# Hybrid decoder layer: the first up-projection weights are cast behind the last tiles of h, and two output-weight tiles change places

## The chip, the cores and the metric

The kernel runs on one core of one Trainium2 chip. The metric is the device time of one execution in microseconds (us); less is better. The engines are named as in the profile: PE is TensorE (matmuls; PEld its weight loads), DVE VectorE, ACT ScalarE, POOL GpSimd, SP SyncE, which here issues DMAs.

## The reference, cut to what matters

One decoder layer on S = 1024 tokens of width D = 1024, in float32:

```python
xn = rmsnorm(x, attn_norm_g)
proj = xn @ w_in                      # queries, keys, values of two head groups, forget logits
out_a = sliding-window attention with sinks (8 heads)
out_b = forgetting attention (8 heads)
x = x + concat(out_a, out_b) @ w_out  # this sum is h
hn = rmsnorm(x, mlp_norm_g)
x = x + square(relu(hn @ w_up)) @ w_down   # w_up: 1024 x 4096
```

## The kernel before

Everything is kept transposed: a tile of h is 128 of the 1024 features (tile number dt = 0 to 7) by 1024 tokens. The stages are the input projection with both attentions, the output projection, the up projection and the down projection. The scheduler of the framework orders each engine's instructions by a simulated timeline; `tc.issue_after(x)` is a constraint on that order only (what stands under it is put behind x), and each engine then runs its queue in order.

**Split into high and low.** Each float32 factor of a matmul is used as a high part rounded to fp32r and a low part. `split` (line 77) lets ScalarE cast the high part, and line 80 lets VectorE or POOL subtract it from the source. A product of 128 rows of the contraction is then three matmuls: high by high, high by low, low by high (line 73). In the profile `bh` and `bl` are the high and low part of h, `wos` a tile of output weights, `wu` one of up weights.

**Output projection.** `out_first` adds the products of the first four tiles of the attention's output (`mix`) to x for each dt and stores the sum in `part_d`, while the last attention units still run. The second half, over mix 4 to 7, starts with tiles 0 and 4 beside the last attention units and goes on with tiles 1, 5, 2, 6, 3, 7 (the six tiles) when the attention is done. `out_weights` loads a weight tile (`wor`), splits it with ScalarE and POOL, and puts it into one of the places w0 to w6 of the memory, by the counter `i`: tiles 0 and 4 are i = 9 and 10, then tiles 1, 5, 2, 6, 3, 7. A place can be written again when the last reader of what it held is done. `out_finish` (line 982) loads the stored part, adds the product to it (line 988: this is h), stores h to `h_d` (line 989), and splits it. h of tiles 0 to 3 lies in w2, of tiles 4 to 6 in w3, of tile 7 in `rr`. The up projection uses a Strassen-like scheme with seven products n over half-size blocks; their right-hand sides are the halves of h themselves (n = 1, 2, 3: line 977 on ScalarE, 978 on VectorE) and sums `ts` of them (n = 4 to 7: lines 995 and 1007 on VectorE, then `split`). `b12` (line 994) is a scaled copy that those sums use.

**Up projection.** For 16 column blocks j the seven products are made in the order UP = 1, 2, 3, 6, 7, 5, 4, 12 matmuls each, over four contraction tiles k. `up_weights` (line 1048) takes the next place by `w_slot` and splits; the low part is VectorE's for n = 2, 6, 5 and POOL's for n = 1, 3, 7, 4. The weights n = 1 of j = 0 and j = 1 (the first pair) are made ahead of the loop, and their products run first. `up_sum` makes the sums of raw weights (`wus`, lines 1027 and 1030), the loop's end adds the products (`u`, `hb`).

**Attention's last units.** VectorE masks the scores (line 699) with masks `cm` that POOL makes (line 694), ScalarE takes the exponential (line 704), VectorE or POOL divides (lines 713, 715), TensorE transposes the probabilities (`tpb`, line 740), and ScalarE and VectorE split them (`pth`, `ptl`).

Of the kernel before, what the change touches and what calls it, by code (L numbers as in the profile page):

```python
# [9 lines left out]
F32R = mybir.dt.float32r  # L10
BF16 = mybir.dt.bfloat16
AF = mybir.ActivationFunctionType
# [4 lines left out]
P = 128  # L17
# [12 lines left out]
NW = 7  # L30
# [25 lines left out]
def hybrid_layer(  # L56
# [13 lines left out]
    nc = tc.nc  # L70
# [4 lines left out]
    def split(hi, lo, src, hi_eng, lo_eng):  # L75
        if hi_eng is nc.scalar:
            hi_eng.copy(hi, src)  # L77
        else:
            hi_eng.tensor_copy(hi, src)
        return lo_eng.tensor_tensor(out=lo, in0=src, in1=hi.bitcast(F32), op=ALU.subtract)  # L80
# [63 lines left out]
    def slot(tag, name, shape, dt=F32, pool=None):  # L144
        pool = o[pool or ("zx" if tag == "w6" else "zw" if tag[0] == "w" else "zl")]
        return pool.tile([P] + shape, dt, tag=tag, name=name, bufs=1)
# [7 lines left out]
    def x_part(j, k, rows):  # L154

        c, r0 = divmod(rows.start, 512)
        return X[c][k // 2][:, j, k % 2, r0 : r0 + rows.stop - rows.start]
# [27 lines left out]
    for k in range(KT):  # L185
# [18 lines left out]
        for cs in pieces:  # L204
            hi, lo = (x_part(j, k, cs) for j in range(2))
# [657 lines left out]
        mix_tiles(e)  # L863
        return nc.sync.dma_start(mixt[e].bitcast(F32), mixs_d[e].rearrange("c p s -> p c s"))

    WOS = ("w5", "w6", "w0", "w1", "w5", "w6")
    nout = [0]

    def out_weights(dt, e0):
        i = nout[0] = nout[0] + 1  # L870
        wr = o["zw"].tile([P, 4, P], F32, tag="wor", name="wor", bufs=2)
        nc.sync.dma_start(wr, w_o[dt][:, e0 : e0 + 4, :])
        w = slot(WOS[i - 11] if i > 10 else f"w{i % 2}", "wos", [2, 4, P], F32R)
        split(w[:, 0], w[:, 1], wr, nc.scalar, nc.gpsimd)
        return w[:, 0], w[:, 1]

# [11 lines left out]
    def out_products(ps, w, es):  # L888
        wh, wl = w
        for e in es:  # L890
            j = e % 4
            for c in range(2):
                cs = slice(c * 512, (c + 1) * 512)
                mm(ps[c], wh[:, j, :], mh[e][:, cs], j == 0, False)
                mm(ps[c], wh[:, j, :], ml[e][:, cs], False, False)
            for c in range(2):
                cs = slice(c * 512, (c + 1) * 512)
                mm(ps[c], wl[:, j, :], mh[e][:, cs], False, j == 3)
# [73 lines left out]
    left, right = slice(0, 512), slice(512, 1024)  # L972
    part = {}

    def h_split(n, t, src, gain):
        hi, lo = bh[n][:, t, :], bl[n][:, t, :]
        nc.scalar.activation(hi, src, AF.Copy, scale=gain)  # L977
        nc.vector.scalar_tensor_tensor(  # L978
            out=lo, in0=src, scalar=gain, in1=hi.bitcast(F32), op0=ALU.mult, op1=ALU.subtract
        )  # L980

    def out_finish(dt, ps):
        t, gain = dt % 4, gm[:, dt : dt + 1]
        h = slot(f"w{2 + dt // 4}", "h", [S]) if dt < 7 else rr
        with tc.issue_after(part["load"].ins) if dt == 7 else nullcontext():
            part["load"] = nc.sync.dma_start(h, part_d[dt])
        for c, cs in enumerate((left, right)):
            nc.vector.tensor_tensor(out=h[:, cs], in0=ps[c], in1=h[:, cs], op=ALU.add)  # L988
        nc.sync.dma_start(h_d[dt], h)
        if dt < 4:  # L990
            h_split(1, t, h[:, left], gain)
            ts = part["t"] = slot("r1", "ts", [4, 512])
            b12 = part["b12"] = slot("w4", "b12", [512])
            nc.scalar.activation(b12, h[:, right], AF.Copy, scale=gain)
            nc.vector.scalar_tensor_tensor(
                out=ts[:, 0], in0=h[:, left], scalar=gain, in1=b12, op0=ALU.mult, op1=ALU.subtract
            )
            return
        ts, b12 = part["t"], part["b12"]
        h_split(2, t, h[:, left], gain)  # L1000
        h_split(3, t, h[:, right], gain)
        for i, q, other, op in (
            (1, right, ts[:, 0], ALU.add),
            (2, right, b12, ALU.subtract),
            (3, left, ts[:, 1], ALU.subtract),
        ):
            nc.vector.scalar_tensor_tensor(  # L1007
                out=ts[:, i], in0=h[:, q], scalar=gain, in1=other, op0=ALU.mult, op1=op
            )
        part["rest"] = lambda: sum_splits(ts, t, ((0, 5), (3, 4)))  # L1010
        sum_splits(ts, t, ((1, 6), (2, 7)))
        if t < 3:
            part.pop("rest")()

    def sum_splits(ts, t, which):
        for i, n in which:
            split(bh[n][:, t], bl[n][:, t], ts[:, i], nc.scalar, nc.vector)
# [3 lines left out]
    def up_load(j):  # L1021
        raws[j] = slot({0: "m3", 1: "m2"}.get(j, f"r{j % 2}"), "wur", [2, KT, P])
        for i in range(2):
            up_loads[j] = nc.sync.dma_start(raws[j][:, i], w_u[j + i * NJ])

    def minus(out, a, b, eng=nc.vector):
        eng.tensor_tensor(out=out, in0=a, in1=b, op=ALU.subtract)  # L1027

    def plus(out, a, b, eng=nc.vector):
        eng.tensor_tensor(out=out, in0=a, in1=b, op=ALU.add)  # L1030

    def up_sum(j):
        raw = raws.pop(j)
        s = slot("m5" if j % 2 == 0 else "m4" if j > 1 else "r1", "wus", [4, 4, P])
        a11, a12, a21, a22 = raw[:, 0, :4], raw[:, 0, 4:], raw[:, 1, :4], raw[:, 1, 4:]
        plus(s[:, 0], a21, a22)
        minus(s[:, 1], s[:, 0], a11)
        minus(s[:, 2], a11, a21)
        minus(s[:, 3], a12, s[:, 1])
        return {1: a11, 2: a12, 3: s[:, 3], 4: a22, 5: s[:, 0], 6: s[:, 1], 7: s[:, 2]}  # L1040

    nw = [0]

    def w_slot(name, shape, dt=F32):
        nw[0] += 1
        return slot(f"w{(0, 1, 5, 6, 2, 3, 4)[(nw[0] - 1) % NW]}", name, shape, dt)

    def up_weights(n, src):
        w = w_slot("wu", [2, 4, P], F32R)
        split(w[:, 0], w[:, 1], src, nc.scalar, nc.vector if n in (2, 6, 5) else nc.gpsimd)  # L1050
        return w
# [3 lines left out]
    for dt, ps, w in ahead_of:  # L1055
        out_finish(dt, ps)
# [7 lines left out]
    def bank(name):  # L1064
        nbank[0] += 1
        return pm.tile([P, 512], F32, tag=f"m{nbank[0] % 8}", name=name, bufs=1)

    for dt in (1, 5, 2, 6, 3, 7):
        w = out_weights(dt, 4)
        ps = [bank(f"po{c}") for c in range(2)]  # L1070
        out_products(ps, w, range(4, 8))
        out_finish(dt, ps)
        if dt == 5:
            with tc.issue_after(part["load"].ins):
                up_load(1)
        if dt == 3:
            up_ahead = [up_weights(1, up_sums[0][1]), up_weights(1, raws[1][:, 0, :4])]

# [5 lines left out]
    def up_products(n, w, ps):  # L1084
        for k in range(4):
            mm(ps, w[:, 0, k], bh[n][:, k], k == 0, False)
            mm(ps, w[:, 0, k], bl[n][:, k], False, False)
            mm(ps, w[:, 1, k], bh[n][:, k], False, k == 3)
# [3 lines left out]
    def up(j):  # L1092
        if 0 < j < NJ - 1:
            up_load(j + 1)
        src = up_sums.pop(0) if j == 0 else up_sum(j)
        m = {}
        for n in UP:
            if n == 1 and j == 1:
                m[n] = second.pop()
            else:  # L1100
                w = up_ahead.pop(0) if n == 1 and j == 0 else up_weights(n, src[n])
                m[n] = bank(f"pu{n}")
                up_products(n, w, m[n])
            if n == 1 and j == 0:
                second.append(bank("pu1"))
                up_products(1, up_ahead.pop(), second[0])
            if n == 2 and j == 0:
                part.pop("rest")()
            if n == 2 and j == 1:
                nbank[0] += 1  # L1110
            if n == 1:
                u = slot("m1", "u", [4, 512])
                b = slot("m2" if j else "m0", "hb", [4, 512])
                nc.scalar.copy(u[:, 0], m[1])
            if n == 2:
                plus(b[:, 0], m[2], u[:, 0])
            if n == 6:
                plus(u[:, 1], m[6], u[:, 0])
            if n == 7:
                plus(u[:, 2], m[7], u[:, 1])  # L1120
            if n == 5:
                minus(u[:, 3], u[:, 1], m[5])
                minus(b[:, 2], u[:, 2], m[5])
                plus(b[:, 3], m[3], u[:, 3])
            if n == 4:
                plus(b[:, 1], m[4], u[:, 2])
        return lambda: up_end(j, b)
# [207 lines left out]
    for i in range(len(STEPS)):  # L1335
        down(i)
        if STEPS[i][0] == len(PHASES) - 1 and late:
            name, dt, cs = late.pop(0)
# [65 lines left out]
```

## Time and profile before

| | |
|---|---|
| median of 3 runs | 1088.91 us (1088.80 to 1089.02) |
| the profiled execution | 1092.64 us, its span 1090.9 us |
| mean granted TensorE clock | 0.997 |
| PE, PEld busy | 99%, 86% of the span |
| DVE, ACT, POOL busy | 71%, 53%, 36% |
| place A: last attention units | about 397 to 431 us |
| place B: from the output to the up projection | about 460 to 495 us |

In the rows of the trace the first number is the start in us from the span's start, the second the duration in us, then engine, line, operation, output<-inputs, shape and a count (x2: two such in a row in one entry). What stands in brackets is the idle time of the engine just before, and what ended it. A matmul of 128x512 takes 0.39 us from start to end, but the next one starts before it has ended. Rows of the waits give the total in us, how often, and the longest. Names of buffers are cut at their numbers.

### The profile page before, as it was taken

The numbers are of one execution on the slowest core, as the hardware profiler recorded it, in microseconds if no ns is written. First come the engines' busy times: TensorE is split into PE (matmuls) and PEld (weight loads), VectorE is DVE, ScalarE is ACT, GpSimd is POOL, SyncE is SP. The second block draws the span as 40 slices with busy tenths as digits, with TensorE's granted clock in tenths as the row PEclk, the third lists the DMA queues.
The fourth block names the chain that finished last, engine by engine and source line by source line (L and its number), as shares of the span: only waits on it lengthen the run. The fifth ranks groups of instructions, "written<-read, shape, count | busy, mean of one in ns | idle before, by whom it ended". The sixth has DMA issues, their size and how long they took to land.

```text
span 1090.9 us, 15569 instructions
## 1 busy us (share of the span) xinstructions
PE 1074.9 (99%) x5492; PEld 933.1 (86%) x5492; DVE 773.2 (71%) x1319; ACT 577.0 (53%) x1022; POOL 388.8 (36%) x350
## 2 busy tenths in 40 slices
PE   9999999999999999989999999999999999999998
PEld 8999999999998887868888888888888888888886
DVE  7377787877866787887776759665675876664395
ACT  5558587776867765545545453443533433333331
POOL 4572433547456653233332232332222232131100
PEclk9999999999999999999999999999999999999999
DMA  8401112334747664643545443443998895665523
GB/s 281 168 19 57 62 46 62 116 99 128 253 155 248 230 196 169 220 172 142 193 167 202 174 164 117 147 172 145 331 390 311 308 327 190 218 234 185 176 88 115
DMA packets 96222, 195.67 MB, mean 179 GB/s; under 512 B 7392, under 2 KB 19856, under 8 KB 96144
## 3 DMA queue, kind: packets, MB, share of 16 engines
q1 hardware_dynamic: 95856, 194.54, 51.6%
q8 instruction: 43, 0.70, 0.3%
q14 instruction: 35, 0.29, 0.1%
q10 hardware_dynamic: 288, 0.15, 0.0%
HBM read 141.61 MB, written 53.04 MB: 178 GB/s over the span
## 4 chain that ended last, share of the span: by engine, by line
PE 67%; DVE 4%; DMA 3%; issue 1%; ACT 1%; SPq 0%; DVEq 0%; ACTq 0%
PE pu L73 28%; PE pd L73 28%; PE po L73 4%; PE pvb L73 2%; PE tpb L740 2%; PE spb L73 1%; DMA mix_d<-mtb 1%; PE ps L73 1%; DMA h<-part_d 1%; DMA h_d<-h 1%; DVE h L988 1%; DVE bl L978 0%; DVE ptl L403 0%; DVE ts L1007 0%; DMA mixn<-rd_d 0%
## 5 line engine op out<-in xcount | busy, mean ns | idle before, releaser
L73 PE MATMUL pd<-hx,wx 128*128 128x512 f32 (+1 forms) x1350 | 304.9, 388 | 0.0
L73 PEld LDWEIGHTS pd<-hx,wx 128*128 128x128 f32 x1350 | 252.7, 188 | 52.2
L73 PE MATMUL pu<-bh,wu 128*128 128x512 f32 x896 | 277.9, 391 | 3.6 <-ACT bh L977 3.6
L73 PEld LDWEIGHTS pu<-bh,wu 128*128 128x128 f32 x896 | 169.0, 189 | 39.4 <-ACT bh L977 4.0
L73 PE MATMUL ps<-w,x 128*128 128x384 f32 (+1 forms) x960 | 196.5, 342 | 1.1 <-POOL w L80 0.8
L73 PE MATMUL pu<-bl,wu 128*128 128x512 f32 x448 | 175.2, 391 | 0.2 <-DVE bl L978 0.2
L73 PEld LDWEIGHTS ps<-w,x 128*128 128x128 f32 x960 | 165.1, 188 | 5.3 <-POOL w L80 1.5
L77 ACT CAST hx<-hr 128x1024 fp32r<-128x1024 f32 x56 | 59.0, 1054 | 174.9 <-PE pd L73 170.6
L80 POOL TENSOR_TENSOR wx<-wda,wx 128x1024 fp32r<-128x1024 f32 x24 | 66.1, 2755 | 194.8 <-ACT wx L77 172.4
L80 DVE TENSOR_TENSOR hx<-hr,hx 128x1024 fp32r<-128x1024 f32 x56 | 77.4, 1387 | 75.7 <-ACT hx L77 75.7
L73 PEld LDWEIGHTS pu<-bl,wu 128*128 128x128 f32 x448 | 84.5, 189 | 18.3 <-DVE bl L978 0.7
L80 POOL TENSOR_TENSOR wu<-wus,wu 128x512 fp32r<-128x512 f32 x32 | 48.0, 1502 | 130.5 <-ACT wu L77 130.5
L73 PE MATMUL po<-mix,wos 128*128 128x512 f32 x384 | 93.4, 393 | 0.0
L73 PEld LDWEIGHTS po<-mix,wos 128*128 128x128 f32 x384 | 70.7, 188 | 14.0 <-ACT pc L916 0.2
L77 ACT CAST wu<-wus 128x512 fp32r<-128x512 f32 x64 | 39.3, 620 | 80.7 <-PE pu L73 73.2
L80 POOL TENSOR_TENSOR wu<-wur,wu 128x512 fp32r<-128x512 f32 x32 | 47.0, 1469 | 86.5 <-ACT wu L77 86.5
L1027 DVE TENSOR_TENSOR ht<-hb 128x512 f32<-128x512 f32 x32 | 22.9, 757 | 64.1 <-ACT hb L1131 64.1
L704 ACT ACTIVATE sb<-sb,nmb 128x128 f32<-128x128 f32 (+3 forms) x64 | 49.8, 779 | 26.8 <-DVE nmb L699 26.1
L403 DVE TENSOR_TENSOR ptl<-tpb,pth 128x512 fp32r<-128x512 f32 (+1 forms) x80 | 50.1, 631 | 18.3 <-ACT pth L402 17.9
L77 ACT CAST wx<-wda 128x1024 fp32r<-128x1024 f32 x56 | 58.5, 1049 | 8.1 <-DMA wda<-in_w_d_dram 8.1
L80 POOL TENSOR_TENSOR w<-wr,w 128x384 fp32r<-128x384 f32 (+1 forms) x47 | 49.9, 1069 | 29.6 <-ACT w L77 15.8
L694 POOL TENSOR_SCALAR_AFFINE_SELECT cm<-cb 128x128 f32<-128x128 f32 (+1 forms) x64 | 30.8, 482 | 60.2 <-DVE nmb L699 59.6
(205 smaller groups left out, 1829.9 us busy)
## 6 DMA issues: line engine op xcount, KB each, us to landing
wda<-in_w_d_dram SPq DMA_DIRECT2D x34, 1024.0 KB, 9.2
hr<-hid_d SPq DMA_DIRECT2D x56, 512.0 KB, 5.8
wur<-in_w_u_dram SPq DMA_DIRECT2D x32, 512.0 KB, 4.4
hid_d<-ht SPq DMA_DIRECT2D x16, 1024.0 KB, 4.4
hid_d<-hb SPq DMA_DIRECT2D x16, 768.0 KB, 3.9
mix<-mixs_d SPq DMA_DIRECT2D x7, 1024.0 KB, 5.7
wr<-in_w_b_dram SPq DMA_DIRECT2D x32, 192.0 KB, 2.5
xq<-in_x_dram SPq DMA_DIRECT2D x8, 512.0 KB, 5.8
```

The source lines that it names most:

```text
L73: return nc.tensor.matmul(out, lhsT, rhs, start=start, stop=stop)
L77: hi_eng.copy(hi, src)
L80: return lo_eng.tensor_tensor(out=lo, in0=src, in1=hi.bitcast(F32), op=ALU.subtract)
L403: nc.vector.tensor_tensor(out=lo[:, cols], in0=pt[:, cols], in1=hi[:, cols].bitcast(F32), op=ALU.subtract)
L694: nc.gpsimd.affine_select(out=cm, in_=bias, pattern=[[-1, n]], compare_op=ALU.is_ge, fill=BIG, base=n - P, channel_multiplier=1,)
L704: nc.scalar.activation(pr[:, :nk], pr[:, :nk], AF.Exp, scale=-1.0, bias=nm[:, c : c + 1], accum_out=dn_b[p % 2][:, h, i : i + 1] if p < 3 ...
L740: nc.tensor.transpose(tp[:, c0 : c0 + P], probs[qi][:, kb * P : (kb + 1) * P], ident)
L988: nc.vector.tensor_tensor(out=h[:, cs], in0=ps[c], in1=h[:, cs], op=ALU.add)
L1027: eng.tensor_tensor(out=out, in0=a, in1=b, op=ALU.subtract)
```

## The change

There are three edits.

1. The table WOS gets another entry in front and is read from i = 10 on. Tile 4's weights (i = 10) go to w5, which is free, where they went to w0, which tile 7's first-half weights hold; tile 1's go to w0 instead of w5; tile 5's stay in w6, tile 2's in w0 go to w1, tile 6's to w5, tile 3's to w0, tile 7's stay in w6.
2. `out_finish` keeps its last cast on ScalarE of lines 977 and 994, one for each of the six tiles in a list `casts`. In the loop's first block (j = 0) the weights of n = 2 are put behind tile 3's copy b12, and all the others behind tile 7's cast of the right half (n = 3).
3. The order of places in `w_slot` changes: the first pair uses w1 and w5, n = 2 w0, n = 3 w6, n = 6 w3 (was w2), n = 7 w4 (was w3), n = 5 w2 (was w4), n = 4 w1 (the cycle then repeats).

```diff
@@ -863,14 +863,14 @@
         mix_tiles(e)
         return nc.sync.dma_start(mixt[e].bitcast(F32), mixs_d[e].rearrange("c p s -> p c s"))
 
-    WOS = ("w5", "w6", "w0", "w1", "w5", "w6")
+    WOS = ("w5", "w0", "w6", "w1", "w5", "w0", "w6")
     nout = [0]
 
     def out_weights(dt, e0):
         i = nout[0] = nout[0] + 1
         wr = o["zw"].tile([P, 4, P], F32, tag="wor", name="wor", bufs=2)
         nc.sync.dma_start(wr, w_o[dt][:, e0 : e0 + 4, :])
-        w = slot(WOS[i - 11] if i > 10 else f"w{i % 2}", "wos", [2, 4, P], F32R)
+        w = slot(WOS[i - 10] if i > 9 else f"w{i % 2}", "wos", [2, 4, P], F32R)
         split(w[:, 0], w[:, 1], wr, nc.scalar, nc.gpsimd)
         return w[:, 0], w[:, 1]
 
@@ -974,7 +974,7 @@
 
     def h_split(n, t, src, gain):
         hi, lo = bh[n][:, t, :], bl[n][:, t, :]
-        nc.scalar.activation(hi, src, AF.Copy, scale=gain)
+        part["cast"] = nc.scalar.activation(hi, src, AF.Copy, scale=gain)
         nc.vector.scalar_tensor_tensor(
             out=lo, in0=src, scalar=gain, in1=hi.bitcast(F32), op0=ALU.mult, op1=ALU.subtract
         )
@@ -991,7 +991,7 @@
             h_split(1, t, h[:, left], gain)
             ts = part["t"] = slot("r1", "ts", [4, 512])
             b12 = part["b12"] = slot("w4", "b12", [512])
-            nc.scalar.activation(b12, h[:, right], AF.Copy, scale=gain)
+            part["cast"] = nc.scalar.activation(b12, h[:, right], AF.Copy, scale=gain)
             nc.vector.scalar_tensor_tensor(
                 out=ts[:, 0], in0=h[:, left], scalar=gain, in1=b12, op0=ALU.mult, op1=ALU.subtract
             )
@@ -1043,7 +1043,7 @@
 
     def w_slot(name, shape, dt=F32):
         nw[0] += 1
-        return slot(f"w{(0, 1, 5, 6, 2, 3, 4)[(nw[0] - 1) % NW]}", name, shape, dt)
+        return slot(f"w{(1, 5, 0, 6, 3, 4, 2)[(nw[0] - 1) % NW]}", name, shape, dt)
 
     def up_weights(n, src):
         w = w_slot("wu", [2, 4, P], F32R)
@@ -1065,6 +1065,7 @@
         nbank[0] += 1
         return pm.tile([P, 512], F32, tag=f"m{nbank[0] % 8}", name=name, bufs=1)
 
+    casts = []
     for dt in (1, 5, 2, 6, 3, 7):
         w = out_weights(dt, 4)
         ps = [bank(f"po{c}") for c in range(2)]
@@ -1073,6 +1074,7 @@
         if dt == 5:
             with tc.issue_after(part["load"].ins):
                 up_load(1)
+        casts.append(part["cast"].ins)
         if dt == 3:
             up_ahead = [up_weights(1, up_sums[0][1]), up_weights(1, raws[1][:, 0, :4])]
 
@@ -1098,7 +1100,8 @@
             if n == 1 and j == 1:
                 m[n] = second.pop()
             else:
-                w = up_ahead.pop(0) if n == 1 and j == 0 else up_weights(n, src[n])
+                with tc.issue_after(casts[-2 if n == 2 else -1]) if j == 0 else nullcontext():
+                    w = up_ahead.pop(0) if n == 1 and j == 0 else up_weights(n, src[n])
                 m[n] = bank(f"pu{n}")
                 up_products(n, w, m[n])
             if n == 1 and j == 0:
```

What this makes of the queues is shown at three places. In the names of the queues wos_5732 is tile 4's weights, wos_5913 tile 1's; wu_6142 and wu_6145 are the first pair, wu_6223 is n = 2 of j = 0, wu_6244 n = 3, wu_6260 n = 6, wu_6277 n = 7, wu_6294 n = 5, wu_6313 n = 4; h_6131 is h of tile 3, rr_5866 of tile 7; ts_6045 and ts_6138 are the sums of tiles 6 and 7 (with 2 and 3). In a piece of the difference, - stands before, + after.

ScalarE at place B, behind the last casts of tile 6's sums:

```order
 L77 CAST bh4_5864<-ts_6045 128x512
-L77 CAST wu_6277<-wus_5901 128x512
-L77 CAST wu_6223<-wur_5867 128x512
 L977 ACTIVATE bh1_5852<-h_6131,vt_65 128x512
 L994 ACTIVATE b12_6139<-h_6131,vt_65 128x512
+L77 CAST wu_6223<-wur_5867 128x512
 L77 CAST bh5_5862<-ts_6138 128x512
+L977 ACTIVATE bh2_5854<-rr_5866,vt_65 128x512
+L977 ACTIVATE bh3_5856<-rr_5866,vt_65 128x512
 L77 CAST wu_6244<-wus_5901 128x512
-L977 ACTIVATE bh2_5854<-rr_5866,vt_65 128x512
```

The two casts of weights that stood ahead of tile 3's cast of h now stand behind it; n = 7's (wu_6277) moves far down, behind tile 7's casts, and tile 7's two casts move ahead of n = 3's.

POOL at place B, its subtractions of up weights:

```order
 L80 TENSOR_TENSOR wu_6142<-wur_5867,wu_6142 128x512
 L80 TENSOR_TENSOR wu_6145<-wur_6004,wu_6145 128x512
-L80 TENSOR_TENSOR wu_6277<-wus_5901,wu_6277 128x512
 L80 TENSOR_TENSOR wu_6244<-wus_5901,wu_6244 128x512
 L80 TENSOR_TENSOR wu_6313<-wur_5867,wu_6313 128x512
+L80 TENSOR_TENSOR wu_6277<-wus_5901,wu_6277 128x512
 L80 TENSOR_TENSOR wu_6400<-wus_6342,wu_6400 128x512
```

n = 7 was the first of the three behind the pair, and is now the last, behind n = 4.

POOL at place A, between two subtractions of mix:

```order
 L80 TENSOR_TENSOR mixs_5426<-mixr_5319,mixn_5320 128x512
-L80 TENSOR_TENSOR wos_5913<-wor_5911,wos_5913 128x512
 L694 AFFINE_SELECT cm_5589<-cb31_5144 128x256
 L715 TENSOR_TENSOR sb_5569<-sb_5569,dnb_5571 128x128
 L694 AFFINE_SELECT cm_5637<-cb31_5144 128x128
 L715 TENSOR_TENSOR sb_5583<-sb_5583,dnb_5585 128x256
+L694 AFFINE_SELECT cm_5655<-cb31_5144 128x256
 L917 TENSOR_TENSOR xt_5530<-xt_5530,pc_5563 128x512 x2
-L694 AFFINE_SELECT cm_5655<-cb31_5144 128x256
-L80 TENSOR_TENSOR wos_5732<-wor_5730,wos_5732 128x512
+L80 TENSOR_TENSOR wos_5913<-wor_5911,wos_5913 128x512
 L80 TENSOR_TENSOR mixs_5524<-mixr_5324,mixn_5325 128x512
```

Tile 1's subtraction takes the place that tile 4's had, tile 4's is gone from here (it stands further up), and the last unit's mask cm_5655 moves ahead of the two additions of x.

## The prediction

> **What bounds the kernel now.** I read the page first, then TensorE's waits, then the rows and the granted clock around its two long waits.
>
> ```profile
> span 1090.9 us, 15569 instructions
> PE 1074.9 (99%) x5492; PEld 933.1 (86%) x5492; DVE 773.2 (71%) x1319; ACT 577.0 (53%) x1022; POOL 388.8 (36%) x350
> ```
> ```profile
> PE pu L73 <- ACT bh L977: 3.6, 1, 3.6
> PE tpb L740 <- DVE ptl L403: 2.6, 1, 2.6
> PE qps L73 <- DVE warm L181: 1.3, 1, 1.3
> ...
> PE pu L73 <- DVE bl L978: 0.2, 1, 0.2
> ```
>
> TensorE is busy for 99% of the span, so only what makes TensorE wait, or run at half clock, can be won. The two long waits are the two places that this change touches: 3.6 + 0.2 us where the up projection begins (place B), 2.6 us in the last attention units (place A). Place B on TensorE:
>
> ```profile
> 469.13 0.39 PE L73 MATMUL pu<-bh,wu 128*128 128x512 f32 x1
> 469.36 0.39 PE L73 MATMUL pu<-bl,wu 128*128 128x512 f32 x1
> ...
> 470.94 0.39 PE L73 MATMUL pu<-bh,wu 128*128 128x512 f32 x1
> 474.91 0.72 PE L73 MATMUL pu<-bh,wu 128*128 128x512 f32 x2 [3.58 <-ACT bh L977]
> ...
> 476.32 0.80 PE L73 MATMUL pu<-bl,wu 128*128 128x512 f32 x1 [0.22 <-DVE bl L978]
> ...
> 480.07 0.39 PE L73 MATMUL pu<-bl,wu 128*128 128x512 f32 x1
> ```
>
> Starts at full clock are 0.227 us apart (469.13 to 469.36, and 469.13 to 470.94 in 8 steps). The matmul at 480.07 is the 23rd; without a loss it would start at 469.13 + 22 x 0.227 = 474.12. So place B costs 5.95 us, of which 3.80 is waiting. The rest is in the clock (first numbers: length, then TensorE busy; the number behind the engines is the granted clock):
>
> ```profile
> 418.20:421.60 3.40, 0.84 (x7) 0.60 (x7) 3.33 (x6) 2.34 (x5) 0.74 (x1) 1.00 0.85 234
> 421.74:425.15 3.41, 3.41 (x19) 3.39 (x16) 1.54 (x3) 1.94 (x4) 0.00 (x0) 0.50 0.34 91
> 469.52:472.94 3.42, 1.81 (x8) 1.15 (x7) 2.71 (x5) 0.37 (x1) 0.00 (x0) 1.00 0.98 376
> 472.94:476.35 3.41, 1.23 (x5) 0.71 (x5) 2.09 (x3) 2.38 (x4) 1.27 (x1) 1.00 0.86 351
> 476.35:479.76 3.41, 3.41 (x8) 2.74 (x9) 3.33 (x5) 2.80 (x5) 1.29 (x1) 0.50 0.01 2
> ```
>
> A stretch of 3.41 us in which TensorE was busy for 1.23 or 0.84 us is followed by one at half clock, and one with 1.81 us busy is not. A stretch at half clock does half its work, so it costs 3.41 / 2 = 1.7 us.
>
> What makes TensorE wait at B is ScalarE's queue, and behind it a store:
>
> ```profile
> 469.27 0.62 ACT L77 CAST bh<-ts 128x512 fp32r<-128x512 f32 x1 [1.37 <-DVE ts L1007]
> 473.09 0.62 ACT L77 CAST wu<-wus 128x512 fp32r<-128x512 f32 x1 [3.20 <-DMA h_d<-h]
> 473.62 0.61 ACT L77 CAST wu<-wur 128x512 fp32r<-128x512 f32 x1
> 474.14 0.72 ACT L977 ACTIVATE bh<-h,vt 128x512 fp32r<-128x512 f32 x1
> 474.76 0.71 ACT L994 ACTIVATE b<-h,vt 128x512 f32<-128x512 f32 x1
> ```
> ```profile
> 466.57 6.42 DMA h_d<-h
> ```
> ```profile
> 470.35 1.29 DVE L988 TENSOR_TENSOR h<-po,h 128x512 f32<-128x512 f32 x2
> 471.55 0.69 DVE L80 TENSOR_TENSOR bl<-ts,bh 128x512 fp32r<-128x512 f32 x1
> 474.26 1.34 DVE L80 TENSOR_TENSOR wu<-wur,wu 128x512 fp32r<-128x512 f32 x1 [2.03 <-ACT wu L77]
> 475.52 0.74 DVE L978 SCALAR_TENSOR_TENSOR bl<-h,vt,bh 128x512 fp32r<-128x512 f32 x1
> ```
>
> The cast at 473.09 is that of the weights n=7. Its place w3 holds tile 6 of h until that tile's store has landed (466.57 + 6.42 = 472.99). Behind it in ScalarE's queue stand the cast of n=2 and the cast of tile 3's h (bh at 474.14), for which TensorE waits, though that h was ready when the first of the two adds at 470.35 ended, at about 471.03.
>
> **The change, part by part.** No instruction is added or removed, and no store or load; the order and the places change.
>
> *Casts of h first, n=7 in w4 and late (place B).* The cast of h now stands directly behind the cast at 469.27. It starts at 471.07 and ends at 471.79 (0.72). TensorE's ninth matmul ends its slot at 470.94 + 0.227 = 471.17; it goes on at 471.84 (0.05 behind the cast, as 474.14 + 0.72 to 474.91) and has waited 0.67. VectorE subtracts the low part at 472.15 (one 0.60 slot behind 471.55), until 472.89. The reordered TensorE queue has one matmul for that gap (471.84 to 472.07), goes on at 472.94, and has waited 0.87. Together 1.54 us. Split anyhow over 3.41-us stretches this leaves at least 1.87 us busy, above the 1.81 that was not punished, so I count no half clock. Gain by the end of this product: 5.95 - 1.54 = 4.4 us. Ends: 2.26 if the timed runs had no half clock here (only waiting goes), 4.8 if VectorE takes the low part directly behind the cast (471.84 + 0.74).
>
> *n=2's and n=3's weights, which gave way.* n=2's cast moves behind tile 3's two casts (471.69, 472.35 at the spacing 474.14 to 474.76 of 0.62), so it ends at 472.97 and its low part at VectorE at about 474.1; TensorE reaches n=2 at 472.94 + 0.23 + 13 x 0.227 = 476.1. Covered by 2 us; without the cover it would be the next wait. n=3's cast moves behind both casts of tile 7 and ends at about 477.44; its low part is POOL's, and TensorE asks for it at the third matmul of n=3, in its queue 14 behind n=2's first: 476.1 + 14 x 0.227 = 479.3. VectorE is then in a run of operations without a pause. How POOL fares in one, two rows of each kind tell:
>
> ```profile
> 482.54 6.09 POOL L80 TENSOR_TENSOR wu<-wur,wu 128x512 fp32r<-128x512 f32 x1 [3.08 <-ACT wu L77]
> ```
> ```profile
> 487.40 0.68 DVE L1030 TENSOR_TENSOR hb<-pu,u 128x512 f32<-128x512 f32 x1
> 488.00 1.18 DVE L1030 TENSOR_TENSOR wus<-wur 128x512 f32<-128x512 f32 x1
> ```
> ```profile
> 522.58 1.75 POOL L80 TENSOR_TENSOR wu<-wus,wu 128x512 fp32r<-128x512 f32 x1 [2.96 <-ACT wu L77]
> ```
> ```profile
> 522.50 0.69 DVE L1027 TENSOR_TENSOR wus<-wur 128x512 f32<-128x512 f32 x1
> 523.10 1.78 DVE L1030 TENSOR_TENSOR ht<-hb,ht 128x512 f32<-128x512 f32 x1
> ```
> ```profile
> L80 POOL TENSOR_TENSOR wu<-wus,wu x8: 1267/1320/1754, 473.8 to 529.5; 128x512 fp32r<-128x512 f32 x8
> L80 POOL TENSOR_TENSOR wu<-wur,wu x7: 1290/1299/6087, 457.4 to 518.3; 128x512 fp32r<-128x512 f32 x7
> ```
>
> Undisturbed POOL takes 1.29 us. At 522.58 it waited for VectorE's operation in flight, then VectorE's next was held (1.78 for 0.69). At 482.54 it was kept out until VectorE came to an operation that reads PSUM (487.40), and ended 1.23 behind that start. The last two rows (min, median, max in ns, up to 530 us) show one such loss in 15. I take the first kind: request at 477.5 inside an operation that ends at 478.2, ready at 478.2 + 1.29 = 479.5, so 0.2 late; 0 if VectorE is between two operations, 0.85 if POOL waits for one more. I take 0.3. [...]
>
> *n=4 ahead of n=7 on POOL.* Before, n=7 was done at 475; now its low part stands behind n=4's. VectorE, held once by n=3, ends the sum for tile 7's bh6 at 478.2 + 1.29 + 2 x 0.66 = 480.8; ScalarE's five then follow 0.53 to 0.62 apart: bh6, the copy u, n=4 (ends 482.5), bh7, n=7 (ends 483.6). POOL takes n=4 from 483.0, after the operation in flight, and is ready with n=7's low part at 483.0 + 2 x 1.29 = 485.6; TensorE asks for it at the third matmul of n=7: n=2 from 476.1, then 36 matmuls and two more, 484.8. Wait 0.8; ends 0 (VectorE pauses) and 1.7 (POOL waits for an operation of VectorE before each). This term did not exist before.
>
> *n=5 in w2, n=6 in w3.* w2 holds tile 3's h, whose store is issued here:
>
> ```profile
> 471.66 0.33 SPq L989 DMA_DIRECT2D h_d<-h x1
> ```
>
> With the 6.42 us of the other store it lands at 478.1; n=5's cast is due at 478.5, n=6's in w3 (store landed at 472.99) at 478.0. I count nothing. If the store came 2 us later, n=5's cast would hold ScalarE by as much, and bh6 and n=7 with it: 2 us more on the term before.
>
> *Tile 4's weights earlier, tile 1's later (place A).* Tile 4's cast and POOL subtraction move ahead a long way; tile 1's move behind. Their loads change places on SP's queue; no wait of TensorE above goes back to them, and I count nothing. What holds VectorE here are three operations of POOL, each of which doubles one of VectorE's:
>
> ```profile
> 412.86 2.53 POOL L917 TENSOR_TENSOR xt<-xt,pc 128x512 f32<-128x512 f32 x2 [0.52 <-ACT pc L916]
> ...
> 416.18 1.29 POOL L80 TENSOR_TENSOR wos<-wor,wos 128x512 fp32r<-128x512 f32 x1
> 417.43 1.51 POOL L80 TENSOR_TENSOR mixs<-mixr,mixn 128x512 fp32r<-128x512 f32 x1
> ```
> ```profile
> 414.56 1.39 DVE L624 TENSOR_TENSOR mixr<-mixr,mixn 128x512 f32<-128x512 f32 x1
> ```
>
> After the change a subtraction of weights (now tile 1's) stands at the same place between the same two neighbours, so all three remain. The mask and the probabilities of the last unit move ahead of them, but the list of VectorE operations up to the one TensorE waits for is the same, and it ran without a pause from 414.56. Ends: 0.8 us worse (one more operation held) to 1.3 better (one held fewer), and with a wait under 1.6 us the half clock at 421.74 goes too. I take 0.15 better.
>
> *Sum:* 4.4 - 0.3 - 0.8 + 0.15 = 3.45 us off. The list of waits has no other of pu, and none of the down projection's pd, so the gain keeps to the end. The profiled execution took 1092.64 (span 1090.9 and 1.74 around it), 3.73 above the median 1088.91; it becomes 1089.2, and the median 1085.5, if the timed runs lose the same at B. They lie within 0.22 us of one another, so they all had the same number of half-clock stretches.
>
> **The rivals.**
>
> 1. *The half clock is not there in the timed runs.* Their median is 3.73 us under the profiled execution, which is two stretches of 1.7 and a little. Then the gain is 3.45 - 1.7 = 1.75: 1087.2. Against it: a wait of 3.58 us leaves one stretch short of work wherever the stretches begin, except when it is cut near its middle. [...]
> 2. [...] If it is kept out as at 482.54, it stays out until VectorE's first operation that reads PSUM, which now stands behind 13 others, at 477.5 + 3 x 0.66 + 10 x 0.60 = 485.5. The low part is done at 485.5 + 1.23 = 486.7; TensorE waits 7.4 us, and a stretch at half clock follows (1.7): 4.4 + 0.15 - 9.1 = -4.55, so 1093.5. It decides once POOL gets in later than about 481: then wait and half clock eat the gain. For it: the run of VectorE is the very one in which the loss occurred. Against it: one loss in 15.
> 3. [...]
> 4. *Place A goes too.* With no operation held twice the wait falls by up to 1.3 and the half clock goes: 3.45 + 1.15 + 1.7 = 6.3 more or less, 1082.6. For it: masks and exponentials are done earlier. Against it: the three POOL operations.
>
> **How the numbers follow.** My forecast has 0.52, the first rival 0.15, the second 0.13, the third 0.11, the fourth 0.06; 0.03 is for none of these. 0.2%, about what a measurement here can tell from no change, is 2.2 us: from 1086.7 to 1091.1. The forecast and the fourth lie on the faster side (0.58 with a little lost to the border), the first and most of the third within it, the second and a share of the third beyond. The forecast's own range is 1083.5 (4.8, no wait behind it, and 0.6 at A) to 1086.7. For 8 in 10 the range goes up to the third rival, 1091.3, and down to 1083.0, and leaves out the second and fourth.
>
> **What would show it.** Right: TensorE's wait on ScalarE's bh at line 977 falls from 3.6 to about 0.7, one on VectorE's bl rises to about 0.9, no stretch at half clock follows, and ScalarE has no wait for a store of h near 470. POOL's subtraction of n=3 starts near 477.5 and takes under 2 us. A wait of TensorE on POOL's wu of under 1 us each at n=3 and n=7. At 420 the wait on ptl stays above 2 us. Wrong: a POOL subtraction of wu of 5 us or more with TensorE waiting for it; a wait of TensorE on n=2's weights; a cast of wu that waits for a store of h; or a clock of 1.00 throughout in the profile with no gain.

## The result and the profile after

Over 18 runs of each the changed kernel took 1086.64 us (median, 1084.97 to 1088.97), the kernel before 1089.65 (1087.27 to 1093.64): a ratio of 0.9970, 95% interval 0.9963 to 0.9978, or 3.3 us less (2.4 to 4.0). A second series gave 1086.17 against 1089.40, 0.9974 (0.9964 to 0.9984). The forecast was 3.45 us less: 1085.5, with a range of 1083.5 to 1086.7, counted from the 1088.91 of 3 runs. 1086.64 lies at the slow end of that range. The profiled execution took 1086.83 us. TensorE's waits in it, and the rows of place B:

```profile
span 1085.1 us, 15578 instructions
PE 1072.6 (99%) x5492; PEld 932.6 (86%) x5492; DVE 780.5 (72%) x1319; ACT 574.3 (53%) x1022; POOL 384.2 (35%) x350
```
```profile
PE pu L73 <- ACT bh L977: 1.2, 1, 1.2
PE tpb L740 <- DVE ptl L403: 1.0, 1, 1.0
...
PE tpb L740 <- DVE dnb L711: 0.6, 1, 0.6
PE pu L73 <- DVE bl L978: 0.6, 1, 0.6
```
```profile
465.25 0.39 PE L73 MATMUL pu<-bh,wu 128*128 128x512 f32 x1
...
467.06 0.39 PE L73 MATMUL pu<-bh,wu 128*128 128x512 f32 x1
468.68 0.49 PE L73 MATMUL pu<-bh,wu 128*128 128x512 f32 x1 [1.23 <-ACT bh L977]
469.78 0.50 PE L73 MATMUL pu<-bl,wu 128*128 128x512 f32 x1 [0.61 <-DVE bl L978]
```

The waits of 3.6 and 0.2 us at place B have become 1.23 and 0.61; the 2.6 us at place A have become 0.6 and 1.0. ScalarE shows why at B: tile 3's cast of h stands directly behind the last cast of a sum, and no cast waits for a store any more.

```profile
466.09 0.62 ACT L77 CAST bh<-ts 128x512 fp32r<-128x512 f32 x1 [1.37 <-DVE ts L1007]
467.90 0.72 ACT L977 ACTIVATE bh<-h,vt 128x512 fp32r<-128x512 f32 x1 [1.19 <-DVE h L988]
468.56 0.72 ACT L994 ACTIVATE b<-h,vt 128x512 f32<-128x512 f32 x1
469.19 0.60 ACT L77 CAST wu<-wur 128x512 fp32r<-128x512 f32 x1
```

POOL takes n = 3, n = 4 and n = 7, and VectorE's operations beside it are the long ones:

```profile
474.33 1.30 POOL L80 TENSOR_TENSOR wu<-wus,wu 128x512 fp32r<-128x512 f32 x1 [12.81 <-ACT wu L77]
477.02 1.64 POOL L80 TENSOR_TENSOR wu<-wur,wu 128x512 fp32r<-128x512 f32 x1 [1.40 <-ACT wu L77]
478.62 1.74 POOL L80 TENSOR_TENSOR wu<-wus,wu 128x512 fp32r<-128x512 f32 x1
```
```profile
474.33 2.50 DVE L978 SCALAR_TENSOR_TENSOR bl<-rr,vt,bh 128x512 fp32r<-128x512 f32 x2
...
477.42 3.48 DVE L80 TENSOR_TENSOR wu<-wus,wu 128x512 fp32r<-128x512 f32 x2
```

With POOL idle two operations of VectorE took 1.41 us (line 978, at 463.99) and 1.29 us (line 80, at 465.98) in this profile; these take 2.50 and 3.48. POOL itself took 1.64 and 1.74 us at the most (1.29 undisturbed), so it never lost more than 0.5 us, and TensorE has no wait on POOL at B.

**Half clock.** This profile has one stretch at half clock behind B and none behind A; another, at the very end of the run, comes after TensorE's last matmul (length, then TensorE busy; the number behind the engines is the granted clock):

```profile
414.40:417.80 3.40, 2.10 (x15) 1.62 (x13) 3.40 (x7) 2.49 (x7) 2.12 (x2) 1.00 0.75 275
...
467.67:471.08 3.41, 1.79 (x7) 1.27 (x8) 3.32 (x7) 2.51 (x4) 0.00 (x0) 1.00 1.02 419
471.08:474.49 3.41, 3.41 (x10) 2.67 (x9) 3.37 (x6) 2.08 (x4) 0.16 (x1) 0.50 0.64 259
```

**Where two profiles mislead.** TensorE's order of matmuls is nearly the same in both kernels, so the start of its 2401st, 2651st and 3001st matmul marks places in the program. The two profiled executions differ by 5.8 us, but 1.6 of it stands before the 2401st, where the programs are alike; 2.3 lies in place A (2401st to 2651st: 46.07 to 43.77 us) and 1.9 in place B (2651st to 3001st: 85.31 to 83.37). From the 3001st to the last both take 564.30 us. By these two profiles A had given more than B, against the forecast (0.15 and 3.3). The first experiments tell whether that is so.

### The profile page after: what moved, and what is told of

It is laid out like the page before. It is cut to its first block, busy times and chain, and to the rows that moved or that the text cites. A ratio compares the mean times of both kernels' runs of the same rounds, so it can differ in the third digit from the quotient of the medians.

```text
span 1085.1 us, 15578 instructions
## 1 busy us (share of the span) xinstructions
PE 1072.6 (99%) x5492; PEld 932.6 (86%) x5492; DVE 780.5 (72%) x1319; ACT 574.3 (53%) x1022; POOL 384.2 (35%) x350
## 4 chain that ended last, share of the span: by engine, by line
PE 90%; DVE 4%; DMA 2%; issue 1%; ACT 1%; POOL 1%; SPq 0%; ACTq 0%; DVEq 0%
PE pu L73 28%; PE pd L73 28%; PE ps L73 13%; PE po L73 7%; PE pvb L73 3%; PE spb L73 3%; PE tpb L740 3%; PE sp L73 1%; PE tpa L565 1%; PE pv L73 1%; DMA xq<-in_x_dram 1%; DMA wr<-in_w_a_dram 1%; PE ptk L331 1%; PE ptq L331 1%; DVE x L207 1%
## 5 line engine op out<-in xcount | busy, mean ns | idle before, releaser
L80 DVE TENSOR_TENSOR hx<-hr,hx 128x1024 fp32r<-128x1024 f32 x56 | 72.3, 1300 | 71.0 <-ACT hx L77 71.0
L80 POOL TENSOR_TENSOR wu<-wur,wu 128x512 fp32r<-128x512 f32 x32 | 43.0, 1344 | 91.5 <-ACT wu L77 91.5
```

## The experiments

The kernels of one series ran on one chip beside the kernel before, which took 1090.06 us (32 runs) in the first series, 1089.40 (18) in the second, 1090.51 (12) in the third.

**Edit 1 alone.** The output weights' new places; the up weights' places turned so far that the first pair and n = 2 fit, the casts as before.

```diff
-    WOS = ("w5", "w6", "w0", "w1", "w5", "w6")
+    WOS = ("w5", "w0", "w6", "w1", "w5", "w0", "w6")
-        w = slot(WOS[i - 11] if i > 10 else f"w{i % 2}", ...)
+        w = slot(WOS[i - 10] if i > 9 else f"w{i % 2}", ...)
-        return slot(f"w{(0, 1, 5, 6, 2, 3, 4)[...]}", ...)
+        return slot(f"w{(1, 5, 0, 6, 2, 3, 4)[...]}", ...)
```

> Edit 1 alone: tile 4's output weights in w5 and ahead, tile 1's in w0; of the up weights' places only the first three are turned so that the first pair and n = 2 follow the output tiles as before, and casts at place B stand as before. Theory 1 (the two profiles): place A gives 2.3 us by itself (its wait falls from 2.6 to about 1.0 + 0.6 and the stretch at half clock behind it goes), so about 1087.3 against 1089.6, and place B still waits 3.6 us for bh. Theory 2 (the split of the prediction): place A gives 0.15 us, about 1089.5, and the wait on ptl stays above 2 us.

Measured: 1089.04 us, ratio 0.9992 (0.9981 to 1.0004). TensorE's waits:

```profile
PE pu L73 <- ACT bh L977: 3.1, 1, 3.1
PE qps L73 <- DVE warm L181: 1.3, 1, 1.3
PE tpb L740 <- DVE ptl L403: 1.0, 1, 1.0
...
PE tpb L740 <- DVE dnb L711: 0.7, 1, 0.7
```

The mechanism of theory 1 at A is there (waits of 1.0 and 0.7 us, no half clock behind them), and 3.1 us at B remain. The size is 0.9 us, with an interval of 2.1 less to 0.4 more: it excludes theory 1's 2.3 and allows theory 2's 0.15, whose wait of over 2 us is not there. So each theory is half right.

**Edits 2 and 3 for place B alone.**

```diff
-        return slot(f"w{(0, 1, 5, 6, 2, 3, 4)[...]}", ...)
+        return slot(f"w{(0, 1, 5, 6, 3, 4, 2)[...]}", ...)
+                with tc.issue_after(casts[-2 if n == 2 else -1]) if j == 0 else nullcontext():
```

> Edits 2 and 3 for place B alone: casts of weights behind the casts of h, n = 6, 7, 5 in w3, w4, w2; output weights as before. Theory 1: about 2 us, 1087.6: the wait for bh falls to 0.7 to 1.2 us, that for bl is 0.6 to 0.9, and a stretch at half clock follows in most runs. Theory 2: 3.3 us, 1086.3: the same waits, but no half clock in most runs. Place A keeps its 2.6 us in both.

Measured: 1086.88 us, 0.9971 (0.9959 to 0.9984): 3.2 us, nearly the whole gain. That is theory 2's size; the interval, 1.7 to 4.5 us, also allows the 2 us of theory 1. Waits:

```profile
PE tpb L740 <- DVE ptl L403: 2.1, 1, 2.1
...
PE pu L73 <- DVE bl L978: 1.1, 2, 0.6
PE pu L73 <- ACT bh L977: 1.0, 1, 1.0
```

A kept a wait of 2.1 us and had no stretch at half clock this time; B had none either. So most of the gain is B's.

**Without the order of the casts.**

```diff
-                with tc.issue_after(casts[-2 if n == 2 else -1]) if j == 0 else nullcontext():
+                with nullcontext():
```

> The changed kernel without the constraint on the order of casts (edit 2 undone, edits 1 and 3 kept). n = 6's cast, now in w3, and n = 2's stand ahead of tile 3's cast of h. Theory 1 (the order behind a place that waits for a store is what costs): place B's wait for bh is back at 3 to 3.8 us, with n = 6 in the place of n = 7; the time is that of edit 1 alone, about 1087.3. Rival (the new places alone do it): as the changed kernel, 1086.6, with a wait for bh of about 1.2.

Measured: 1089.78 us, 0.9992 (0.9981 to 1.0003): the gain is gone. ScalarE:

```profile
463.70 0.63 ACT L77 CAST bh<-ts 128x512 fp32r<-128x512 f32 x1 [1.36 <-DVE ts L1007]
467.56 0.62 ACT L77 CAST wu<-wus 128x512 fp32r<-128x512 f32 x1 [3.24 <-DMA h_d<-h]
468.09 0.61 ACT L77 CAST wu<-wur 128x512 fp32r<-128x512 f32 x1
468.61 0.72 ACT L977 ACTIVATE bh<-h,vt 128x512 fp32r<-128x512 f32 x1
```

n = 6 has taken n = 7's place in w3, and in the queue in front of tile 3's h; TensorE waits 3.5 us for bh. Theory 1 holds in its mechanism. The time is that of edit 1 alone (1089.04) within the intervals, though both are slower than the 1087.3 that was expected of them.

**The order without the new places of n = 6, 7, 5.**

```diff
-        return slot(f"w{(1, 5, 0, 6, 3, 4, 2)[...]}", ...)
+        return slot(f"w{(1, 5, 0, 6, 2, 3, 4)[...]}", ...)
```

> The changed kernel with the places of n = 6, 7, 5 as before (w2, w3, w4; edit 3 kept for the first pair, n = 2 and n = 3 alone). With the constraint on the order, n = 7's cast stands behind tile 7's two casts of h and behind n = 3's, when the store of w3 has long landed. Theory 1 (the order of the casts does it): as the changed kernel, 1086.6, with waits of 1.2 for bh and 0.6 for bl. Rival (the places do it): the wait for the store is back in front of something that TensorE needs, and the time is 1 to 3 us longer.

Measured: 1087.23 us, 0.9982 (0.9973 to 0.9991), beside the changed kernel's 0.9974 (0.9964 to 0.9984) in the same series. Its waits are 0.9 for bh, 0.6 and 0.5 for bl, and one new one of 0.3 us for n = 6's low part. No cast of its ScalarE waits for a store at B. So the order of the casts brings about two thirds of the gain by these ratios (2.0 us of 2.8). Whether the places add the 1 us between the two medians the runs leave open; in the profiles place B takes as long with the old places (82.85 us) as with the new (82.39 to 83.37, table below).

**The changed kernel again,** for its clock:

> The changed kernel once more, beside the others on one chip. Theory 1 (the runs so far: place B alone moved the time by 3.1 us, place A alone by 0.9): 3.0 to 3.4 us less than before, most of it at B. Its mean granted clock: if the change takes away one stretch at half clock on average, as the first runs of it and of before suggest, the time lost to half clock is 1.7 us less than before's; if the stretch at B stays, as in its first profile, it is the same within 0.5 us.

Measured: 1086.17 us, as above. Its profile has no stretch at half clock at all but the one at the very end of the run, where TensorE has done its work. Counted back from that one in steps of 3.413 us, the stretches at place B are these:

```profile
464.90:468.31 3.41, 2.16 (x11) 1.46 (x9) 3.41 (x7) 1.52 (x3) 0.00 (x0) 1.00 0.92 320
468.31:471.73 3.42, 2.81 (x12) 2.08 (x13) 3.33 (x6) 1.62 (x3) 0.00 (x0) 1.00 1.00 411
```

The waits of 1.3 and 0.6 us at the start of B, nearly those of the first profile, fell into two stretches here, and nearly all into one there (1.79 us of work).

The mean granted clock over the runs of this series is 0.9972 before and 0.9989 after, so 1.8 us less of the span lost to half clock ((1 - clock) x span: 3.02 against 1.22). For place B alone, beside its own runs of before, it is 1.6 us (3.44 against 1.81). The clocks are recorded to three decimals, so these are rough: about half of the gain is the clock, the rest the shorter waits.

**What is late next: the pair interleaved.** On top of the changed kernel, the nine matmuls of the pair's second product over tiles 0 to 2 go ahead of those of both products over tile 3 (`up_products` gets the range of tiles as an argument `ks`; that piece is left out here):

```diff
-                up_products(n, w, m[n])
-            if n == 1 and j == 0:
-                second.append(bank("pu1"))
-                up_products(1, up_ahead.pop(), second[0])
+                if n == 1 and j == 0:
+                    second.append(bank("pu1"))
+                    pair = ((w, m[n]), (up_ahead.pop(), second[0]))
+                    for ks in (range(3), range(3, 4)):
+                        for wp, ps in pair:
+                            up_products(1, wp, ps, ks)
+                else:
+                    up_products(n, w, m[n])
```

> The changed kernel with the 9 matmuls of the second of the first pair over tiles 0 to 2 put ahead of those over tile 3 of both: 2.04 us of work for TensorE in the gap in which it waits 1.2 + 0.6 us. Theory 1 (VectorE is late next): the waits for bh and bl of n = 1 go, but TensorE comes to n = 2 2 us earlier than VectorE has bl of tile 7 (475.0 against 473.0 by the profile of the changed kernel), so waits of 1 to 2 us on bl appear at n = 2 and n = 6; gain 1 to 1.5 us on the changed kernel, about 1085.3. Rival (that wait is all): 1.84 us and the stretch at half clock go, 3.5 us, about 1083.1.

Measured: 1086.21 us, 0.9967 (0.9952 to 0.9983), no clear difference from the changed kernel: the 1 to 1.5 us of theory 1 are not shown, and the rival's 3.5 us are excluded. The wait on bl is at n = 2, as theory 1 said; the other is not at n = 6 but earlier, for n = 3's weights.

```profile
469.91 0.50 PE L73 MATMUL pu<-bl,wu 128*128 128x512 f32 x1 [0.42 <-DVE bl L978]
...
474.44 0.50 PE L73 MATMUL pu<-bh,wu 128*128 128x512 f32 x1 [0.63 <-ACT wu L77]
476.34 0.50 PE L73 MATMUL pu<-bl,wu 128*128 128x512 f32 x1 [1.40 <-DVE bl L978]
```

**Those two moved ahead:** the cast of n = 3's weights on ScalarE, and tile 7's low parts on VectorE, on top of the interleaved pair.

```diff
-                with tc.issue_after(casts[-2 if n == 2 else -1]) ...
+                with tc.issue_after(casts[-2 if n in (2, 3) else -1]) ...
-        nc.vector.scalar_tensor_tensor(out=lo, ...)
+        part["low"] = nc.vector.scalar_tensor_tensor(out=lo, ...)
+            with tc.issue_after(part["low"].ins) if dt == 7 else nullcontext():
                 nc.vector.scalar_tensor_tensor(out=ts[:, i], ...)
```

> The kernel with the pair's matmuls interleaved, with two more moves: n = 3's cast may stand behind tile 3's copy as n = 2's does (ScalarE waited 1.4 us there), and tile 7's low parts bl of n = 2 and 3 stand ahead of its sums on VectorE. Theory 1 (VectorE's order was late next): the waits of 0.6 for n = 3's weights and 1.4 for bl at n = 2 go, 0.4 for bl of n = 1 stays, and the time falls by 1.5 to 2 us against the interleaved kernel, to about 1084.5. Rival (VectorE as a whole is late, its order does not matter): the wait of 1.4 us comes back at n = 6 or n = 7, whose sums are now later, and the time stays at 1086.

Measured: 1084.16 us, 0.9957 (0.9944 to 0.9969), 5.2 us less than before and 2.0 less than the changed kernel beside it (1086.17). In its profile TensorE's only wait at B is

```profile
473.14 0.50 PE L73 MATMUL pu<-bl,wu 128*128 128x512 f32 x1 [0.20 <-DVE bl L978]
```

and POOL takes n = 3 at 470.81, beside VectorE's two additions that read PSUM (rr at 470.86), where neither is longer than alone (1.29 and 1.28 us):

```profile
470.81 1.29 POOL L80 TENSOR_TENSOR wu<-wus,wu 128x512 fp32r<-128x512 f32 x1 [10.04 <-ACT wu L77]
476.33 2.97 POOL L80 TENSOR_TENSOR wu<-wus,wu 128x512 fp32r<-128x512 f32 x1 [4.23 <-DVE wu L80]
```
```profile
470.86 1.28 DVE L988 TENSOR_TENSOR rr<-po,rr 128x512 f32<-128x512 f32 x2
```

So it was the order on VectorE and ScalarE, not VectorE's load. What each of the two moves gave, and whether they need the interleaving, was not tried. The second POOL row took 1.7 us more than the first, beside VectorE's operations at 476.20 and 476.86 (0.75 us, and 1.29 for two), as the one at 482.54 before the change took 4.8 us more (6.09), but nobody waited for it.

**The last kernel with the old output weights,** to weigh A where B has no wait left:

```diff
-    WOS = ("w5", "w0", "w6", "w1", "w5", "w0", "w6")
+    WOS = ("w5", "w6", "w0", "w1", "w5", "w6")
-        return slot(f"w{(1, 5, 0, 6, 3, 4, 2)[...]}", ...)
+        return slot(f"w{(0, 1, 5, 6, 3, 4, 2)[...]}", ...)
```

> The last kernel (pair interleaved, n = 3's cast and tile 7's low parts ahead) with tile 4's and tile 1's output weights at their old places and in their old order. Theory 1 (place A's order is worth next to nothing, as its stretches in the profiles say: 44.1 us with the old order and 43.7 to 44.5 with the new): within 0.9 us of 1084.2. Rival (edit 1 is worth the 2.3 us that the first two profiles show): 1086.5.

Measured: 1085.48 us, 0.9954 (0.9938 to 0.9971), against 0.9957 (0.9944 to 0.9969) for the kernel with the new ones, each beside its own runs of before on its own chip. By itself 1085.48 lies between theory 1 (up to 1085.1) and its rival (1086.5); by the ratios no difference is shown. With both intervals about 1.9 us stay possible, so the 2.3 us are excluded and the 1.2 of the table below are not. The clocks lean to some gain at A: 2.63 us lost to half clock per run here, 0.87 in the five runs with the new ones, and this profile has its 2.6 us of wait at A with a half clock behind it.

**The kernel before, two more profiles.**

> The kernel before once more, for its profile. Theory 1: the stretch at half clock behind place A is a matter of where the wait falls: it is there in some profiles and not in others, with the same wait of 2 to 2.6 us, and place A takes 46.1 us with it and 44.1 to 44.4 without; place B takes 85 us with its stretch. Rival: it is always there with the old order.

> As the run before it: the kernel before a third time, for its profile.

Measured: 1090.23 and 1089.96 us in one run each. The first has its wait of 2.6 us at A and no half clock behind it, as theory 1 had it: the wait fell into two stretches (counted back from its stretch at half clock at B).

```profile
415.23:418.64 3.41, 2.27 (x16) 1.87 (x14) 3.41 (x7) 1.81 (x4) 2.98 (x3) 1.00 0.80 300
418.64:422.06 3.42, 1.98 (x15) 1.75 (x16) 2.69 (x6) 1.89 (x5) 0.00 (x0) 1.00 0.76 231
```

The second has 2.1 us at A with a half clock, and two stretches in a row at B:

```profile
415.35:418.76 3.41, 1.45 (x11) 1.23 (x12) 2.88 (x7) 2.09 (x6) 0.11 (x1) 1.00 0.90 275
418.76:422.17 3.41, 3.41 (x20) 3.41 (x18) 2.29 (x5) 1.92 (x4) 0.00 (x0) 0.50 0.32 58
466.55:469.96 3.41, 1.32 (x6) 0.75 (x4) 3.18 (x6) 0.62 (x1) 0.00 (x0) 1.00 1.01 358
469.96:473.37 3.41, 1.21 (x3) 1.01 (x4) 1.85 (x2) 2.37 (x4) 1.27 (x1) 0.50 0.96 393
473.37:476.80 3.43, 3.43 (x10) 2.66 (x9) 3.35 (x6) 2.58 (x5) 1.30 (x1) 0.50 0.02 6
```

The time between the marked matmuls in all profiles that are alike at the place:

| place | order | us in each profile (* with a stretch at half clock, ** two) | mean |
|---|---|---|---|
| A | old | 46.07*, 44.91, 45.33*, 44.12, 45.94* | 45.27 |
| A | new | 43.77, 44.27, 44.51, 44.21, 43.74, 43.85, 43.99 | 44.05 |
| B | old casts | 85.31*, 84.78*, 86.08**, 84.81*, 84.72* | 85.14 |
| B | new casts | 83.37*, 82.63, 82.39, 82.85 | 82.81 |
| B | pair interleaved | 82.97 | |
| B | and two moves | 80.25, 80.33 | 80.29 |

By these means B gives 2.3 us, A 1.2; together 3.5, against 3.3 (first runs) and 2.8 (second series, by its ratio) measured. The runs of place B alone gave 3.2 (1.7 to 4.5), which holds the 2.3.

## Why the prediction was right

- *Place B's cause* was right in every part that was tried: the cast of n = 7 behind a store, in front of tile 3's h. With the order undone another cast stands there and the wait is back; with the old places and the new order the gain stays for the most part.
- *The waits at B* were forecast at 0.67 and 0.87 us and are 1.23 and 0.61. The reordered queue did what was said (VectorE's low part one slot behind), but tile 3's h came later against TensorE: its additions started at 467.18, 1.93 us behind the first matmul of pu; before they started 1.22 behind (470.35 and 469.13). VectorE's chain there takes the same 5.85 us in both (464.50 to 470.35, 461.33 to 467.18), so it began later. Why is not shown. TensorE's lead from A is not the reason: with the new casts the distance is 1.62 to 1.96 us in four profiles, 1.70 in the one with the old output weights; with edit 1 alone it is 1.07. The old casts have 1.07 to 1.22 in four profiles and 2.18 in a fifth. Against matmuls 0.227 us apart, the 206 from the first of pu to the 3001st lose 5.9 us before and 4.0 and 3.2 in the two profiles of the changed kernel (the 4.0 with its half clock), where the forecast leaves 1.54 + 0.3 + 0.8 = 2.6.
- *No half clock at B* holds in three of four profiles. In the fourth a stretch with 1.79 us of work was punished; I had put the border between 1.23 and 1.81. The step that failed is the size of the waits: with 1.23 + 0.61 us a stretch can be left with 1.57, where I had counted on 1.87 at the least. That three profiles escaped is the luck of where the stretches began: 0.16 and 3.57 us behind the first matmul of pu in the second profile of the changed kernel (464.90 and 468.31, against 464.74), 2.42 behind it in the first (467.67, against 465.25).
- *Terms that did not occur:* 0.3 us at n = 3 and 0.8 at n = 7. POOL took at most 0.5 us more than its 1.29 each time, and TensorE never waited for it; in three of the four profiles with the new casts it waited 0.5 us for bl at n = 2 instead, in the second profile of the changed kernel behind two operations of VectorE that took 2.50 us beside a subtraction of POOL (at 473.86 and 473.85). The second and third rival, in which POOL is kept out as at 482.54 for n = 3 (1093.5) or for n = 4 and n = 7 (1090.9), did not come; that a loss is possible near this place the kernel with the two moves shows (2.97 us). My chance for them, one loss in 15, counted as an accident what belongs to the order: the subtraction that took 6.09 us at 482.54 took 6.10 in each of the three other profiles with the same order there (before twice more, edit 1 alone).
- *Place A* was forecast at 0.15 and is 1.2 by the profiles: this term was mis-sized. I wrote that all three operations of POOL remain in the way. One no longer was: POOL's subtraction of mix started later and was itself the one to wait.

```profile
416.60 1.93 POOL L80 TENSOR_TENSOR mixs<-mixr,mixn 128x512 fp32r<-128x512 f32 x1 [1.28 <-ACT mixn L77]
```
```profile
416.46 0.40 DVE L80 TENSOR_TENSOR mix<-mtb,mix 64x256 fp32r<-64x256 f32 x1
416.79 0.60 DVE L713 TENSOR_SCALAR sb<-sb,dnb 128x768 f32<-128x768 f32 x1
```

  VectorE's subtraction there (416.46) took 0.40 us; in the profile of the kernel before it took 1.21:

```profile
416.54 1.21 DVE L80 TENSOR_TENSOR mix<-mtb,mix 64x256 fp32r<-64x256 f32 x1
```

  What is left of the wait is cut into 0.6 and 1.0 us, and none of the seven profiles with the new order has a stretch at half clock behind it, where three of five with the old order have. Most of A's 1.2 us is that: the two old ones without it have a mean of 44.5, 0.5 above the new. Timed alone it is not clear of no change.
- *The total*, 3.3 for 3.45, is in part luck: by the profiles the forecast was too high at B (2.3 for 3.3) and too low at A (1.2 for 0.15), and the two nearly cancel. The first rival (no half clock in the timed runs, 1087.2) is wrong in its reason: the granted clock of the runs shows 1.8 us less lost.
- *The three runs of before* agreed within 0.22 us, and I took from it that all runs have the same number of stretches at half clock. That was an accident: the 18 runs span 6.4 us, and the clocks of before in the later series go from 0.998 to 0.995, which is 2.2 to 5.4 us lost, by my estimate one to three stretches of 1.7 us.

## What to carry to other kernels

A cast that waited 3.20 us for a place to be free held everything behind it on ScalarE, and TensorE for 3.58 us: put the work that the bound engine waits for ahead of it, and let the work with slack wait. Once the first wait is gone, look at the next product's inputs on every engine before moving more work; filling the gap on TensorE brought nothing until two inputs were moved, and then 2 us. Take the effect of one place from several profiles or from a kernel with that edit alone, since two single profiles put the larger share at the wrong place.

## What the runs showed of the hardware

The half clock fell on a grid in these runs, with an edge between 1.79 and 1.81 us of work in a stretch. In each trace the stretches at half clock begin whole steps of 3.413 us apart (in that of before at 421.74, 476.35 and 1090.75: 16 and 180 steps). On each trace's own grid, between 40 and 1075 us, the twelve profiles have ten stretches in which TensorE was busy for 0.27 to 1.79 us, and each is followed by half clock; none with 1.81 us or more is. So the same wait of 2.6 us at A had half clock behind it in one profile, where it left 0.93 us of work in one stretch, and not in another, where it was shared out (2.27 and 1.98). The grid is not fixed to the program: behind the first matmul of pu a stretch begins after 2.42 us in one profile of the changed kernel, after 0.16 and 3.57 in the other, and the timed runs of before in the first series span 6.8 us (1087.12 to 1093.87) though their work is the same.

What a meeting of POOL and VectorE cost went with what VectorE read in these profiles: POOL's 1.29 us beside two additions from PSUM (1.28 us) cost nothing on either side, while two of VectorE's operations with both inputs in SBUF took 2.50 us beside a subtraction of POOL (1.41 with POOL idle). Which of the two took longer went with the order of the instructions (POOL's 6.09 to 6.10 us in four of four profiles with the same order); what decides it the runs do not show.
